# First pass of a two-layer encoder: tokens transposed by products with a diagonal of their roots, c spread from eight columns

## The chip, the cores and the metric

The kernel runs on one core of one Trainium2 chip. The metric is the device time in microseconds of one execution, from a set of three runs; lower is better. One execution was also taken by the hardware profiler, which gives the rows quoted here.

Five engines of the core work side by side, each in the order of its own queue: TensorE (PE in the rows; PEld is its weight load), VectorE (DVE), ScalarE (ACT), GpSimd (POOL), and SyncE (SP), whose queue issues nearly all the DMAs.

## The reference

A trunk of two layers over 1024 tokens of width 1024, in f32. Layer 0 is a differential attention, layer 1 a latent attention. Each layer is modulated by a vector c. What matters here is how a layer begins:

```python
def _rmsnorm(x, g):
    xf = x.astype(jnp.float32)
    y = xf * lax.rsqrt(jnp.mean(xf * xf, axis=-1, keepdims=True) + RMS_EPS)
    return (y * g.astype(jnp.float32)).astype(x.dtype)

def _modulation(c, ada_w, ada_b):
    mod = jax.nn.silu(c) @ ada_w + ada_b
    shift, scale, gate = jnp.split(mod[:, None, :], 3, axis=-1)
    return shift, scale, gate

for i in range(DEPTH):
    shift, scale, gate = _modulation(c, ada_w[i], ada_b[i])
    h = _rmsnorm(x, norm_g[i]) * (1.0 + scale) + shift
    y = mixer_i(h, ...)          # begins with proj = h @ w_in
    x = x + gate * y
return _rmsnorm(x, final_norm_g)
```

Each token of x is multiplied by its own root, `y = rsqrt(mean(x^2) + eps)`, then each feature by `a = g * (1 + scale)`, and `b = shift` is added. The change touches only how h of layer 0 comes about.

## The kernel before

Tokens lie on partitions when x is loaded (`xs0`: four tiles of 128 tokens x 1024 features, the first half of the tokens; `xs1`: the second half). The products need h with features on partitions, so x goes through TensorE in eight chunks of 128 features. `h_chunk` (L478) makes one chunk for 512 tokens: four transposes into one PSUM bank (`trh`, or `trc` in a wide bank), then ScalarE reads the bank twice, as `h * a + b` rounded to the short format of the products (`h0h`) and once more in f32, and GpSimd subtracts the two to get the remainder `h0l` (in the second half VectorE makes the f32 copy). Every f32 product is done as three products of such pairs (high x high, high x low, low x high).

The work at the start, in stages:

- **The vector c.** It is loaded as one row (`crow`, L565), goes through tanh on ScalarE and one step on VectorE (L600, L601), and is spread over all partitions by two products with a row of ones into the PSUM bank `cb` (L605). `keep_busy` (L559) issues products of ones with ones before and after it: 8, then 9 (`WARM`, L64).
- **The modulation.** For chunk k, `mod_pair` (L441) has VectorE multiply two loaded tiles of the ada weight (512 KB each, tag `ada`, four slots) with `cb` and sum each over its row; a third small step (L447) makes `a = (a + 1) * g`.
- **The roots.** The squares of the four x tiles are summed on ScalarE and VectorE, GpSimd takes the power, and ScalarE scales the first 256 columns of each x tile in place (L618, L621; `X_CUT`). VectorE scales the other 768 columns later (`x_rest`, L623), two tiles behind the modulation of chunk 0 and two behind that of chunk 1.
- **The first pass** (loop at L661, k from -1 to 8): `h_chunk` of chunk k stands ahead of the 15 products of chunk k - 1 (`SKEW`): eight for v with h0h, two for k, then five with h0l. The sums stay in the banks `vacc` and `kacc`. In between VectorE works out the rotary angles and ScalarE their sines.
- **The q strip** (L736): 24 products for the first half of the tokens; its bank comes free when the first `vacc` has been stored (L375: a ScalarE copy and a VectorE subtraction).
- **The second pass** (loop at L741): the second half of the tokens, whose four x tiles were scaled in place by `norm_x` (L468) and L730 to L733; `h_chunk` runs three chunks ahead (`SKEW1`) of twelve products per chunk.

The order on each engine is mostly that of the program; `tc.issue_after(x)` puts instructions behind x on their engine. The weights of v, k and q arrive in f32 and are split into high (ScalarE) and low (GpSimd or VectorE) parts as they are needed.

Of the kernel before, what the change touches and what calls it, by code (L numbers as in the profile page):

```python
# [11 lines left out]
F32 = mybir.dt.float32  # L12
# [9 lines left out]
P = 128  # L22
# [9 lines left out]
_W = [("norm_g0", KT), ("ada_bsh0", KT), ("ada_bsc0", KT), ("norm_g1", KT), ("ada_bsh1", KT),  # L32
      ("ada_bsc1", KT), ("subln_g", 1), ("q_a_norm_g", 3), ("kv_a_norm_g", 2), ("inv", 1), ("ada_bg0", KT), ("ada_bg1", KT)]
VEC, NVEC = {}, 0
# [27 lines left out]
X_ACT0 = (0, 2)  # L62
X_CUT = 256
WARM = (8, 9)  # L64
SIN_AT = (4, 5, 7)
# [16 lines left out]
def trunk(ctx: ExitStack, tc: tile.TileContext, A, out):  # L82
# [358 lines left out]
    def mod_pair(l, j, ws, c_):  # L441

        g, bsh, bsc, a_, b_ = mods[l]
        js = slice(j, j + 1)
        mod_dot(ws[0], bsh[:, js], b_[:, js], c_)
        mod_dot(ws[1], bsc[:, js], a_[:, js], c_)
        return V.scalar_tensor_tensor(out=a_[:, js], in0=a_[:, js], scalar=1.0, in1=g[:, js], op0=ALU.add, op1=ALU.mult).ins  # L447

# [28 lines left out]

    def h_chunk(l, xn4, k, dst, hp, sub=G, wide=False, act=False, f32=None):  # L478

        _, _, _, a_, b_ = mods[l]  # L480
        if wide:
            tr = bank("cb", "trc", [P, D])[:, :HF].rearrange("p (j q) -> p j q", j=4)
        else:
            tr = bank("tr", "trh", [P, 4, P])
        for j in range(len(xn4)):
            nk = KT // len(xn4[j])
            PE.transpose(tr[:, j, :], xn4[j][k // nk][:, (k % nk) * P : (k % nk + 1) * P], ident)
# [4 lines left out]
        h_chunk.act = S.activation(hh, tr[:, :n, :], AF.Identity, bias=bk, scale=ak).ins  # L492
# [69 lines left out]

    crow = p1.tile([P, D], F32, name="crow", tag="ada", bufs=ADA_B)
    th = p1.tile([P, D], F32, name="cth", tag="ada", bufs=ADA_B)
    SP.dma_start(crow[0:1, :], A["c"])  # L565
    xs0 = [load_x(0, 0)]
# [32 lines left out]

    c_act = S.activation(th[0:1, :], crow[0:1, :], AF.Tanh, scale=0.5).ins  # L600
    c_last = V.scalar_tensor_tensor(out=crow[0:1, :], in0=th[0:1, :], scalar=1.0, in1=crow[0:1, :], op0=ALU.add, op1=ALU.mult).ins  # L601
    cb = bank("cb", "cb", [P, D])
    for f in range(2):
        fs = slice(f * HF, f * HF + HF)
        spread = PE.matmul(cb[:, fs], ones[0:1, :], crow[0:1, fs], start=True, stop=True).ins  # L605
    with tc.issue_after(spread):
        keep_busy(WARM[1])
    c2 = pg.tile([P, D], F32, name="c2")

    y0 = [None] * 4  # L610
    ss0 = sm.tile([P, 4], F32, name="xss")
# [4 lines left out]
    for j in range(3):  # L616
        y0[j] = y_[:, j : j + 1]
        S.mul(xs0[j][0][:, :X_CUT], xs0[j][0][:, :X_CUT], y0[j])  # L618
    sq_halves([xs0[3][0][:, :HF], xs0[3][0][:, HF:]], ss0[:, 3:4])
    y0[3] = inv_rms(ss0[:, 3:4], 1)[:, 0:1]  # L620
    h_chunk.act = S.mul(xs0[3][0][:, :X_CUT], xs0[3][0][:, :X_CUT], y0[3]).ins  # L621

    def x_rest(j):  # L623
        V.tensor_scalar(xs0[j][0][:, X_CUT:], xs0[j][0][:, X_CUT:], y0[j], None, op0=ALU.mult)

# [35 lines left out]
    for k in range(-1, KT + SKEW):  # L661
        if k + 1 < KT:
# [12 lines left out]
            if k >= 0:  # L675
                with tc.issue_after(m_last):
                    next(angle_steps, None)
        if k < 0:
            with tc.issue_after(m_last):
                x_rest(0)  # L680
                x_rest(1)
        if k == 0:
            with tc.issue_after(m_last):
                x_rest(2)
                x_rest(3)
        if k == X1_AT:
# [8 lines left out]
        if 0 <= k < KT:  # L695
            h_chunk(0, xs0, k, h0[k][0], p1, act=True)
            if k % 4 == 0:
# [25 lines left out]
    with tc.issue_after(h_chunk.act):  # L723
        for j in range(2):
# [3 lines left out]
            V.tensor_add(ssb[:, j : j + 1], ssb[:, j : j + 1], sx)  # L728
    norm_x(ssa, xs1[:2])
    yb = inv_rms(ssb, 2)  # L730
    for j in range(2):
        V.tensor_scalar(xs1[2 + j][0], xs1[2 + j][0], yb[:, j : j + 1], None, op0=ALU.mult)
        S.mul(xs1[2 + j][1], xs1[2 + j][1], yb[:, j : j + 1])  # L733
    load_tables()
# [6 lines left out]
    for k in range(KT + SKEW1):  # L741
        if k < KT:
            if 0 < k <= MODS_K:
                next(mods_g)
            with tc.issue_after(q_split), tc.issue_after(q_mm):
                h_last = h_chunk(0, xs1, k, h0[k][1], p1, V if k in HL_V else G, k % 2 == 1)
        if k >= SKEW1:
# [1684 lines left out]
def layout(inputs):  # L2432
# [4 lines left out]
    def cols(v, n):  # L2437
        return ca(v.reshape(n, P).T)
# [66 lines left out]
```

## Time and profile before

| what | value |
|---|---|
| median of three runs | 1381.4 us (1381.4 to 1382.1) |
| the profiled execution | 1382.89 us |
| its span, first to last instruction | 1380.9 us |
| TensorE busy in the span | 1361.0 us (99%) |
| VectorE, ScalarE, GpSimd busy | 949.2, 738.3, 708.7 us |
| mean granted TensorE clock | 0.995 |
| first product of the first pass | 14.94 us |
| last product of the first pass begins | 48.96 us |
| q strip begins | 50.19 us |
| last transposes before the second pass begin | 55.77 us |
| next strip after the second pass begins | 82.38 us |

The last five rows are from the timeline. A row of the timeline has the start, the duration in us, engine, line, operation, output and input tiles with their shape, a count where like instructions were merged, and in brackets the idle time before it with what ended it. Durations of products overlap: two 128x512 products that each last 0.39 us can start 0.23 us apart. A busy TensorE is therefore not proof of a TensorE at its peak, and the granted clock has to be read beside it.

### The profile page before, as it was taken

To read this page: it belongs to the slowest core of one execution; us is meant where nothing else is said; L and a number is where in the kernel's file an instruction comes from. 1 tells how busy PE (TensorE), PEld (TensorE's weight loads), DVE (VectorE), ACT (ScalarE), POOL (GpSimd) and SP (SyncE) were. 2 spreads that over 40 slices of the span, in tenths; PEclk is the share of its full clock that TensorE was granted. 3 is DMA by queue.
4 is the path that set the end of the run, shared out by engine and by line. 5 is a ranking of instruction groups with operands and counts; after the bars stand their busy time and mean duration, and the time that the engine had idled before them with its cause. 6 is when DMAs were issued, how large, how long until landed. Compare 5 with 4: busy or idle time off the path is not lost.

```text
span 1380.9 us, 20717 instructions
## 1 busy us (share of the span) xinstructions
PE 1361.0 (99%) x7322; PEld 1144.8 (83%) x7322; DVE 949.2 (69%) x1334; ACT 738.3 (53%) x1357; POOL 708.7 (51%) x556
## 2 busy tenths in 40 slices
PE   8999999999999999999999999999999999999997
PEld 6788888888888888887887887788888888888886
DVE  7764788877777767778597987645566555555584
ACT  5633465565655656566648543345454454455554
POOL 4425163647585757565695135532141373834673
PEclk8999999999999999999999999999999999999999
DMA  9867644353444444526654255599343463576373
GB/s 335 275 177 222 211 108 143 113 146 103 156 114 149 135 122 130 153 71 204 210 202 170 60 160 183 161 284 286 115 117 111 111 214 123 190 222 229 118 264 122
DMA packets 149386, 232.06 MB, mean 168 GB/s; under 512 B 20641, under 2 KB 57633, under 8 KB 149282
## 3 DMA queue, kind: packets, MB, share of 16 engines
q1 hardware_dynamic: 149138, 230.48, 53.4%
q8 instruction: 57, 0.93, 0.3%
q14 instruction: 47, 0.39, 0.1%
q10 hardware_dynamic: 144, 0.26, 0.1%
HBM read 144.74 MB, written 61.81 MB: 150 GB/s over the span
## 4 chain that ended last, share of the span: by engine, by line
PE 88%; DVE 4%; DMA 2%; ACT 2%; issue 1%; POOL 1%; SPq 0%; POOLq 0%; DVEq 0%; ACTq 0%
PE s L2109 10%; PE acc L173 9%; PE acc L175 9%; PE acc L174 9%; PE tr L398 8%; PE s L869 8%; PE pv L173 4%; PE pv L174 4%; PE pv L175 4%; PE oy L173 2%; PE oy L174 2%; PE oy L175 2%; PE vps L173 2%; PE vps L174 2%; PE vps L175 2%; PE zacc L175 1%
## 5 line engine op out<-in xcount | busy, mean ns | idle before, releaser
L400 ACT CAST pth<-tr 128x512 fp32r<-128x512 f32 x256 | 150.2, 587 | 279.2 <-PE tr L398 276.3
L401 DVE TENSOR_TENSOR ptl<-tr,pth 128x512 fp32r<-128x512 f32 x256 | 176.3, 689 | 144.6 <-ACT pth L400 143.9
L415 DVE TENSOR_REDUCE nm<-s 128x1 f32<-128x1024 f32 x192 | 234.0, 1219 | 53.7 <-PE s L869 42.9
L219 POOL TENSOR_TENSOR wl<-wraw,wh 128x512 fp32r<-128x512 f32 (+2 forms) x73 | 93.4, 1280 | 264.4 <-ACT wh L218 185.8
L417 ACT ACTIVATE e<-s,nm 128x1024 f32<-128x1024 f32 x128 | 143.7, 1122 | 35.0 <-DVE nm L415 34.4
L398 PE MATMUL tr<-ident,e 128*128 128x128 f32 x1024 | 154.8, 273 | 1.8 <-DVE ptl L401 1.5
L398 PEld LDWEIGHTS tr<-ident,e 128*128 128x128 f32 x1024 | 121.3, 140 | 42.5 <-DVE ptl L401 19.7
L173 PE MATMUL acc<-h0h,wh 128*128 128x512 f32 x360 | 149.5, 415 | 0.0
L173 PE MATMUL pv<-pth,vt 128*128 128x256 f32 x512 | 147.6, 288 | 0.0
L174 PE MATMUL pv<-ptl,vt 128*128 128x256 f32 x512 | 145.4, 284 | 0.0
L175 PE MATMUL pv<-pth,vt 128*128 128x256 f32 x512 | 144.6, 282 | 0.0
L175 PE MATMUL acc<-h0h,wl 128*128 128x512 f32 x360 | 142.0, 394 | 0.0
L174 PE MATMUL acc<-h0l,wh 128*128 128x512 f32 x360 | 141.4, 393 | 0.0
L174 PEld LDWEIGHTS pv<-ptl,vt 128*128 128x128 f32 x512 | 97.5, 190 | 2.5
L1203 POOL TENSOR_TENSOR wol<-wol,woh 128x512 fp32r<-128x512 f32 x56 | 81.9, 1486 | 34.0 <-ACT woh L1202 31.8
L173 PEld LDWEIGHTS pv<-pth,vt 128*128 128x128 f32 x512 | 97.2, 190 | 2.5
L175 PEld LDWEIGHTS pv<-pth,vt 128*128 128x128 f32 x512 | 97.4, 190 | 0.0
L869 PE MATMUL s<-ks,qa 128*128 128x512 f32 x256 | 82.7, 402 | 1.3 <-DVE e L877 1.2
L877 DVE SCALAR_TENSOR_TENSOR e<-s,z,e 128x1024 f32<-128x1024 f32 x64 | 82.2, 1284 | 2.2
L175 PEld LDWEIGHTS acc<-h0h,wl 128*128 128x128 f32 x360 | 67.6, 188 | 14.7
L869 PE MATMUL s<-ks,qb 128*128 128x512 f32 x256 | 79.6, 392 | 0.0
L174 PEld LDWEIGHTS acc<-h0l,wh 128*128 128x128 f32 x360 | 68.2, 189 | 9.2
(433 smaller groups left out, 3416.8 us busy)
## 6 DMA issues: line engine op xcount, KB each, us to landing
ada<-in_ada_ss SPq DMA_DIRECT2D x32, 512.0 KB, 6.1
vS<-v_hl SPq DMA_DIRECT2D x32, 512.0 KB, 5.5
vt<-vS SPq DMA_DIRECT2D x32, 512.0 KB, 4.6
wraw<-in_w_s SPq DMA_DIRECT2D x60, 256.0 KB, 2.8
wol<-tS SPq DMA_DIRECT2D x56, 256.0 KB, 5.3
tS<-ob SPq DMA_DIRECT2D x48, 256.0 KB, 2.2
rp_sw<-rp_raw SPq DMA_DIRECT2D x160, 64.0 KB, 2.0
bc_s<-bc_d SPq DMA_DIRECT2D x34, 256.0 KB, 4.0
```

Of the source, the lines that this page charges most:

```text
L173: PE.matmul(psum, ah, bh, start=first, stop=False, skip_group_check=skip)
L174: PE.matmul(psum, ah, bl, start=False, stop=False, skip_group_check=skip)
L175: mm3.last = PE.matmul(psum, al, bh, start=False, stop=last, skip_group_check=skip).ins
L219: sub = (V if pair_of else G).tensor_sub(l_[:, :n], raw[:, :n], f32v(h_[:, :n]))
L398: transpose_p.last = PE.transpose(tr[:, j, :], p[:, kt * P : (kt + 1) * P], ident).ins
L400: mk["S"] = S.copy(pth[kh][:, :, dst], tr).ins
L401: mk["V"] = V.tensor_sub(ptl[kh][:, :, dst], tr, f32v(pth[kh][:, :, dst])).ins
L415: mk["V"] = V.reduce_max(nm, s_ps, axis=AX.X, negate=True).ins
L417: mk["S"] = S.activation(e, s_ps, AF.Exp, bias=nm, scale=1.0, accum_out=zs).ins
L869: PE.matmul(s_ps[:, kc * HF : (kc + 1) * HF], src[:, c, ql], KS[h][kc][:, c, :], start=fst, stop=not fst)
L877: combined.append(V.scalar_tensor_tensor(out=e0, in0=e1, scalar=z1[:, 0:1], in1=e0, op0=ALU.mult, op1=ALU.add).ins)
L2109: PE.matmul(s_ps[:, kc * HF : (kc + 1) * HF], lhs, rhs(kc), start=i == 0, stop=i == 4)
```

## The change

The constant `c` joins the small vectors that are loaded together as eight columns (`vec`), so its own DMA goes. Its tanh and the step after it work on 128x8 elements. VectorE then scales the identity with each of the eight columns, and TensorE multiplies ones with each of these diagonals, which spreads 128 values of c over all partitions at a time. The second run of `keep_busy` grows from 9 to 15.

x is no longer scaled. In its place ScalarE scales the identity with the roots of each tile of tokens (`diag`, into `dg0` and `dg1`), and `h_chunk` multiplies x with that diagonal instead of transposing it with the identity: the product transposes and scales at once. This is done in both halves of the tokens. `x_rest`, the ScalarE scalings and the `norm_x` of the second half go.

The small step `a = (a + 1) * g` goes from VectorE to ScalarE, as `a * g + g` (`mod_scale`), ahead of each `h_chunk`. After the first chunk's products, three products of ones with ones are issued into `kacc`, which its first real product overwrites.

```diff
-      ("ada_bsc1", KT), ("subln_g", 1), ("q_a_norm_g", 3), ("kv_a_norm_g", 2), ("inv", 1), ...
+      ("ada_bsc1", KT), ("subln_g", 1), ("q_a_norm_g", 3), ("kv_a_norm_g", 2), ("c", KT), ("inv", 1), ...
-X_CUT = 256
-WARM = (8, 9)
+WARM = (8, 15)
+KEEP0 = 3
...
     def mod_pair(l, j, ws, c_):
-        g, bsh, bsc, a_, b_ = mods[l]
+        _, bsh, bsc, a_, b_ = mods[l]
         js = slice(j, j + 1)
         mod_dot(ws[0], bsh[:, js], b_[:, js], c_)
-        mod_dot(ws[1], bsc[:, js], a_[:, js], c_)
-        return V.scalar_tensor_tensor(out=a_[:, js], in0=a_[:, js], scalar=1.0, in1=g[:, js], op0=ALU.add, op1=ALU.mult).ins
+        return mod_dot(ws[1], bsc[:, js], a_[:, js], c_).ins
+
+    def mod_scale(l, j):
+        g, _, _, a_, _ = mods[l]
+        js = slice(j, j + 1)
+        S.activation(a_[:, js], a_[:, js], AF.Identity, bias=g[:, js], scale=g[:, js])
...
-    def h_chunk(l, xn4, k, dst, hp, sub=G, wide=False, act=False, f32=None):
+    def h_chunk(l, xn4, k, dst, hp, sub=G, wide=False, act=False, f32=None, dg=None):
...
-            PE.transpose(tr[:, j, :], xn4[j][k // nk][:, (k % nk) * P : (k % nk + 1) * P], ident)
+            piece = xn4[j][k // nk][:, (k % nk) * P : (k % nk + 1) * P]
+            if dg is None:
+                PE.transpose(tr[:, j, :], piece, ident)
+            else:
+                h_chunk.tr = PE.matmul(tr[:, j, :], piece, dg[:, j, :], start=True, stop=True).ins
...
-    crow = p1.tile([P, D], F32, name="crow", tag="ada", bufs=ADA_B)
-    th = p1.tile([P, D], F32, name="cth", tag="ada", bufs=ADA_B)
-    SP.dma_start(crow[0:1, :], A["c"])
+    cd = p1.tile([P, KT, P], F32, name="cd", tag="ada", bufs=ADA_B)
+    th, cs = [sm.tile([P, KT], F32, name="cth") for _ in range(2)]
...
-    c_act = S.activation(th[0:1, :], crow[0:1, :], AF.Tanh, scale=0.5).ins
-    c_last = V.scalar_tensor_tensor(out=crow[0:1, :], in0=th[0:1, :], scalar=1.0, in1=crow[0:1, :], ...).ins
+    c_act = S.activation(th, part("c"), AF.Tanh, scale=0.5).ins
+    V.scalar_tensor_tensor(out=cs, in0=th, scalar=1.0, in1=part("c"), op0=ALU.add, op1=ALU.mult)
     cb = bank("cb", "cb", [P, D])
-    for f in range(2):
-        fs = slice(f * HF, f * HF + HF)
-        spread = PE.matmul(cb[:, fs], ones[0:1, :], crow[0:1, fs], start=True, stop=True).ins
+    for k in range(KT):
+        c_last = V.tensor_scalar(cd[:, k, :], ident, cs[:, k : k + 1], None, op0=ALU.mult).ins
+        spread = PE.matmul(cb[:, k * P : k * P + P], ones, cd[:, k, :], start=True, stop=True).ins
...
+    dg0 = p1.tile([P, 4, P], F32, name="dg", tag="dg", bufs=1)
+
+    def diag(dst, y):
+        return S.mul(dst, ident, y).ins
...
     for j in range(3):
-        y0[j] = y_[:, j : j + 1]
-        S.mul(xs0[j][0][:, :X_CUT], xs0[j][0][:, :X_CUT], y0[j])
+        diag(dg0[:, j, :], y_[:, j : j + 1])
     sq_halves([xs0[3][0][:, :HF], xs0[3][0][:, HF:]], ss0[:, 3:4])
-    y0[3] = inv_rms(ss0[:, 3:4], 1)[:, 0:1]
-    h_chunk.act = S.mul(xs0[3][0][:, :X_CUT], xs0[3][0][:, :X_CUT], y0[3]).ins
-
-    def x_rest(j):
-        V.tensor_scalar(xs0[j][0][:, X_CUT:], xs0[j][0][:, X_CUT:], y0[j], None, op0=ALU.mult)
+    h_chunk.act = diag(dg0[:, 3, :], inv_rms(ss0[:, 3:4], 1)[:, 0:1])
...
-        if k < 0:
-            with tc.issue_after(m_last):
-                x_rest(0)
-                x_rest(1)
-        if k == 0:
-            with tc.issue_after(m_last):
-                x_rest(2)
-                x_rest(3)
...
         if 0 <= k < KT:
-            h_chunk(0, xs0, k, h0[k][0], p1, act=True)
+            mod_scale(0, k)
+            h_chunk(0, xs0, k, h0[k][0], p1, act=True, dg=dg0)
+            if k == 0:
+                with tc.issue_after(h_chunk.tr):
+                    for _ in range(KEEP0):
+                        PE.matmul(kacc[:, 0:P], ones, ones, start=True, stop=True)
...
-    norm_x(ssa, xs1[:2])
+    ya = inv_rms(ssa, 2)
     yb = inv_rms(ssb, 2)
-    for j in range(2):
-        V.tensor_scalar(xs1[2 + j][0], xs1[2 + j][0], yb[:, j : j + 1], None, op0=ALU.mult)
-        S.mul(xs1[2 + j][1], xs1[2 + j][1], yb[:, j : j + 1])
+    dg1 = p1.tile([P, 4, P], F32, name="dg", tag="dg", bufs=1)
+    for j in range(4):
+        diag(dg1[:, j, :], (ya, yb)[j // 2][:, j % 2 : j % 2 + 1])
...
-                h_last = h_chunk(0, xs1, k, h0[k][1], p1, V if k in HL_V else G, k % 2 == 1)
+                h_last = h_chunk(0, xs1, k, h0[k][1], p1, V if k in HL_V else G, k % 2 == 1, dg=dg1)
...
+    small["c"] = cols(I["c"], KT)
```

More of the change, by code (lines that the diff above doesn't have):

```diff
@@ L32 @@
 _W = [("norm_g0", KT), ("ada_bsh0", KT), ("ada_bsc0", KT), ("norm_g1", KT), ("ada_bsh1", KT),
-      ("ada_bsc1", KT), ("subln_g", 1), ("q_a_norm_g", 3), ("kv_a_norm_g", 2), ("inv", 1), ("ada_bg0", KT), ("ada_bg1", KT)]
+      ("ada_bsc1", KT), ("subln_g", 1), ("q_a_norm_g", 3), ("kv_a_norm_g", 2), ("c", KT), ("inv", 1), ("ada_bg0", KT), ("ada_bg1", KT)]
 VEC, NVEC = {}, 0
@@ L598, in trunk @@
     angle_steps = angles()
-    c_act = S.activation(th[0:1, :], crow[0:1, :], AF.Tanh, scale=0.5).ins
-    c_last = V.scalar_tensor_tensor(out=crow[0:1, :], in0=th[0:1, :], scalar=1.0, in1=crow[0:1, :], op0=ALU.add, op1=ALU.mult).ins
+    c_act = S.activation(th, part("c"), AF.Tanh, scale=0.5).ins
+    V.scalar_tensor_tensor(out=cs, in0=th, scalar=1.0, in1=part("c"), op0=ALU.add, op1=ALU.mult)
     cb = bank("cb", "cb", [P, D])
-    for f in range(2):
-        fs = slice(f * HF, f * HF + HF)
-        spread = PE.matmul(cb[:, fs], ones[0:1, :], crow[0:1, fs], start=True, stop=True).ins
+    for k in range(KT):
+        c_last = V.tensor_scalar(cd[:, k, :], ident, cs[:, k : k + 1], None, op0=ALU.mult).ins
+        spread = PE.matmul(cb[:, k * P : k * P + P], ones, cd[:, k, :], start=True, stop=True).ins
     with tc.issue_after(spread):
@@ L608, in trunk @@
     c2 = pg.tile([P, D], F32, name="c2")
-    y0 = [None] * 4
+    dg0 = p1.tile([P, 4, P], F32, name="dg", tag="dg", bufs=1)
+    def diag(dst, y):
+        return S.mul(dst, ident, y).ins
     ss0 = sm.tile([P, 4], F32, name="xss")
```

## The prediction

> **What bounds the kernel now.** All that is edited runs in the first 83 us of a 1380.9 us span, so I read that stage. First the view of the waits' chain for 0 to 100 us, because it says which work ended last at each point (columns: start us, us, what).
>
> ```profile
> 2.90 6.97 DMA xt<-in_x
> 9.93 7.53 DMA ada<-in_ada_ss
> 17.49 1.28 DVE ada L439
> 18.81 0.99 DVE moda L447
> ...
> 49.55 0.60 DVE v_hl L378
> 50.19 0.50 PE acc L173
> ```
>
> See that the chain is input DMA until 17.49, then almost only VectorE, and TensorE from 50.19 on. Then the table of stretches, by stage: first pass, q strip, second pass (columns: stretch, length, busy us and count of PE, weight loads, DVE, ACT, POOL; granted clock; DMA share; GB/s).
>
> ```profile
> 14.94:49.20 34.26, 34.16 (x148) 27.13 (x148) 32.92 (x54) 20.46 (x33) 22.41 (x18) 0.91 0.94 332
> 50.19:55.77 5.58, 5.58 (x24) 4.57 (x25) 3.86 (x9) 4.37 (x11) 0.85 (x2) 1.00 0.76 203
> 55.77:82.21 26.44, 25.94 (x129) 21.09 (x127) 15.87 (x22) 9.37 (x15) 8.67 (x6) 1.00 0.69 209
> ```
>
> In the first pass TensorE and VectorE are both full, and TensorE has a clock of 0.91. In the second pass TensorE alone is full, at clock 1.00: whatever is added to it there is added to the time. The last chunk of the first pass, and the only breaks of TensorE between the passes and around the second one, from the timeline:
>
> ```profile
> 45.79 0.39 PE L712 MATMUL vacc<-wvh,h0h 128*128 128x512 f32 x1
> ...
> 48.96 0.39 PE L718 MATMUL kacc<-h0l,wh 128*128 128x512 f32 x1
> 50.19 0.50 PE L173 MATMUL acc<-h0h,wq 128*128 128x512 f32 x1 [0.84 <-DVE v_hl L378]
> 57.24 0.50 PE L173 MATMUL vacc<-wvh,h0h 128*128 128x512 f32 x1 [0.43 <-ACT h0h L492]
> 82.38 0.50 PE L173 MATMUL acc<-h0h,wq 128*128 128x512 f32 x1 [0.24 <-DVE v_hl L378]
> ```
>
> The first two rows, 14 steps apart, give the spacing of full-clock products: 3.17 / 14 = 0.226 us.
>
> **The clock.** Cutting the start into stretches of 3.41 us, the spacing at which the granted clock is seen to switch (columns as above):
>
> ```profile
> 0.54:3.95 3.41, 2.90 (x13) 2.90 (x14) 0.53 (x4) 2.34 (x2) 0.50 (x2) 1.00 0.41 106
> 3.95:7.36 3.41, 2.86 (x12) 1.42 (x11) 1.70 (x2) 1.15 (x2) 0.00 (x0) 1.00 0.98 383
> 7.36:10.78 3.42, 3.41 (x17) 3.11 (x15) 1.40 (x6) 1.87 (x4) 0.02 (x1) 0.50 1.02 412
> 10.78:14.20 3.42, 1.31 (x4) 0.55 (x4) 3.11 (x8) 2.31 (x6) 1.60 (x3) 1.00 1.04 405
> 14.20:17.61 3.41, 2.67 (x8) 2.28 (x9) 3.29 (x5) 2.38 (x4) 3.00 (x3) 0.50 1.04 407
> 17.61:21.02 3.41, 3.41 (x9) 2.64 (x8) 3.38 (x7) 1.13 (x2) 2.17 (x2) 0.50 1.03 360
> 21.02:24.43 3.41, 3.41 (x18) 2.79 (x17) 3.38 (x8) 1.18 (x3) 2.55 (x2) 1.00 0.93 312
> ```
>
> Each stretch's clock follows the busy time of the one before: full after 2.90 or 3.41, half after 1.31 (four transposes), still half after 2.67 (some of it transposes); half also after 2.86, of which 1.98 was the c spread from one row. From 14.2 to 21.0 the first chunk's products run at half clock. Later in the kernel two more pairs bound what keeps the clock (PE only: length, busy, clock, DMA share, GB/s):
>
> ```profile
> 847.04:850.45 3.41, 2.13 (x8) 1.00 0.43 161
> 1372.69:1376.10 3.41, 1.25 (x11) 1.00 0.56 208
> 1376.10:1379.51 3.41, 0.00 (x0) 0.50 0.80 297
> ```
>
> After 1.25 busy (37%) the clock falls; after 2.13 (62%) it stays, as no later stretch before 1376 shows less than 1.00.
>
> **What the change costs: products for transposes.** The same shape as the new product (f32, 128x128, a diagonal streamed) is in L926. The price is the time that it takes from its neighbours, against four transposes:
>
> ```profile
> 22.45 0.60 PE L487 MATMUL trh<-ident,xt 128*128 128x128 f32 x4
> 22.81 0.48 PE L713 MATMUL vacc<-wvl,h0h 128*128 128x512 f32 x1
> 23.13 0.39 PE L712 MATMUL vacc<-wvh,h0h 128*128 128x512 f32 x1
> ...
> 1304.75 1.05 PE L926 MATMUL rb<-dg,ones 128*128 128x128 f32 x8
> 1305.56 0.48 PE L173 MATMUL oy<-woh,oah 128*128 128x512 f32 x1
> 1305.87 0.40 PE L174 MATMUL oy<-wol,oah 128*128 128x512 f32 x1
> ```
>
> Four transposes are 4 instructions, four f32 products 8. The third row less one spacing (0.23) less the first: 23.13 - 0.23 - 22.45 = 0.45 us, and 1305.87 - 0.23 - 1304.75 = 0.89. So +0.44 per set of four, eight sets in each pass: +3.5 us of TensorE in each.
>
> Second pass: +3.5, less two breaks that it fills. h0h at 57.24 waits 0.43 behind two sets already issued, and the longer second set fills that; the 0.24 at 82.38 goes, since v_hl comes no later while TensorE does. Net 3.52 - 0.67 = **+2.85**. The norm that goes (products of x with its root on VectorE and ScalarE) lies beside the q strip, which ran to 55.77 without a break, and is worth nothing; the four ScalarE diagonals in its place lie there too.
>
> **First pass, the start.** c comes with vec, so the crow DMA and its issue go, and x is issued 0.33 us earlier; with DMA at 383 to 412 GB/s from 4 us on, all that follows lands about 0.35 earlier. The chain from there:
>
> ```profile
> 1.18 0.33 SPq L565 DMA_DIRECT2D crow<-in_c  x1
> ...
> 11.29 1.28 DVE L439 CUSTOM_DVE_ANT_0 ada<-ada,cb,vec 128x1024 f32<-128x1024 f32 x1 [0.24 <-DMA ada<-in_ada_ss]
> 14.11 0.78 ACT L492 ACTIVATE h0h<-trh,modb,moda 128x512 fp32r<-128x512 f32 x1 [0.23 <-DVE moda L447]
> 14.94 0.80 PE L712 MATMUL vacc<-wvh,h0h 128*128 128x512 f32 x1 [1.18 <-ACT h0h L492]
> 17.27 1.27 POOL L219 TENSOR_TENSOR wl<-wraw,wh 128x512 fp32r<-128x512 f32 x1
> ```
>
> mod_scale moves to ScalarE: 0.2 us there (L952, 128x4: 206 ns) for a VectorE step of 0.16 at 13.85, so even. It waits there for moda, with h0h, h and the next casts queued behind it, but h0h at their head waited for moda already; first product at 14.94 - 0.35 = 14.6. cd holds one ada slot where crow and cth held two, so chunk 1's first ada tile is issued sooner, into DMA queues that are full anyway: nothing. The c spread (eight scalings of 128 columns, above the 0.17 of 128x2 and below the 0.28 of 128x256: I take 0.21, between them, 1.7 in all) begins once vec is there, and is no bound, as ada lands only at 11.27; the eight products, 0.22 each and waited for by the fillers behind them on TensorE's queue, keep pace with it. At either end, 1.4 or 2.2, it is done well before 11.27. The diagonals (0.33 each by L925's 1.4 for four, where the 256-column scalings took 0.44) are ready by 12.6, and h0h waits for moda, not for them.
>
> VectorE loses x_rest and L447:
>
> ```profile
> L439 DVE CUSTOM_DVE_ANT_0 ada<-ada,cb,vec 128x1024 f32<-128x1024 f32 x16 | 20.0, 1274 | 0.7 <-ACT c L637 0.4 <-DMA ada<-in_ada_ss 0.2
> L447 DVE SCALAR_TENSOR_TENSOR moda<-moda,vec 128x1 f32<-128x1 f32 x8 | 4.1, 507 | 0.3
> L624 DVE TENSOR_SCALAR xt<-xt,rq_y 128x768 f32<-128x768 f32 x4 | 3.5, 883 | 0.0
> L925 ACT ACTIVATE dg<-ident,zz 128x128 f32<-128x128 f32 x4 | 1.4, 397 | 0.2 <-DVE zz L2262 0.2
> L952 ACT ACTIVATE sl_w<-zz 128x4 f32<-128x4 f32 x16 | 3.3, 206 | 0.5
> ```
>
> That is 7.6 of its 32.9 us, so it bounds no more; TensorE is late next. Its order: chunk 0 at 14.6; kacc's second product waits for wl, POOL's third job there (18.54 now, about 18.0 then, its two jobs before starting sooner); chunk 1 waits for moda of the ada tile issued at 9.93, which lands about 17.1, so h0h about 19.4. With a full clock chunk 1 starts at 19.5. With half clock until 17.6, those 3.0 us do 1.5 us of the 15 x 0.226 + 0.89 = 4.3 that chunk 0 and the next set hold, and the other 2.8 end at 20.4. Then 7 chunks x 15 x 0.226 = 23.7, and 6 sets x 0.89 = 5.3: end at 48.5 or 49.4 (now 49.2). q then waits only for ScalarE's copy and VectorE's subtraction of the first vacc, about 0.5 after the end, VectorE being free: 49.0 or 49.9, where it is 50.19 now. I take the middle, 49.5, **-0.7**.
>
> Which clock: eight first products as now (full at 3.95), spread and 15 fillers at full clock (0.22 each, 23 in all from 4.2, three instructions after 3.95) end near 9.2; 7.36 to 10.78 is then 54% busy, and 10.78 to 14.20 holds one set (0.89) and the three fills (0.67), 46%. Both lie between the 37% that lost the clock and the 62% that kept it, so both outcomes are priced; at 88% busy from 14.6 it should be back by 17.6. The Trainium skill, page "TensorE: Matmul & The Clock Gate", Part 1, says that the clock drops only after an idle window, which would give 19.5 and a sum lower by 0.4. The 1.25-us stretch above, not idle and yet followed by half clock, speaks against it.
>
> The fills (0.67) and longer warming lie before 14.6 where TensorE has nothing else; if the diagonals came later than 13.5 they would cost up to 0.67.
>
> **Sum.** -0.7 + 2.85 = +2.15 on the span of 1380.9. The profiled run was 1382.89, 1.5 above the median of three runs (1381.4); I add to the median: **1383.6**. Its own range is +1.4 to +3.0: both clocks, and stalls up to 0.5. After 82 us everything waits relative to TensorE's progress, so the delay stays.
>
> **Rivals.**
> Slower: the clock stays half until 21.0 as now, because transitions at 10.78 and 17.61 both go against it. The 6.4 us to 21.0 then do 3.2 of the 4.3, chunk 1 starts at 22.1 instead of 19.9 to 20.0, so +2.2: 1385.8. It decides if 14.2 to 17.6 stays under some 80% busy (2.67 of 3.41 was not enough, 2.90 was). For: waits for wvl and wl there. Against: products count where transposes seem not to. Chance 0.20.
>
> The early gain doesn't come: another feeder than VectorE (ScalarE's table load and sines, wvr landing late; DMA share is 0.94) holds q at 50.2: +2.85, 1384.3. Against: ScalarE is busy 20.5 of 34.3. Chance 0.15.
>
> Faster: a product costs TensorE no more than a transpose here. The first pass then ends at 19.9 + 23.7 + 6 x 0.45 = 46.3, q at 46.8 (-3.4), and the second pass gains 0.24: 1377.8. L926's eight instructions speak against it. Chance 0.07.
>
> Dearer products: at four times a transpose, a set is 1.80, 16 x 1.35 = 21.6 more than 0.45, so about 1401; against it L926's 0.89. Chance 0.02. The Trainium skill's same page, Terms, gives transpose mode as four times faster for FP32; L926 shows two.
>
> A shift that later stages turn into another order of waits, either way by 3 us: 0.06. My forecast keeps 0.50.
>
> **Chances.** A measurement can tell about 0.2% (2.8 us) from no change. Above 1384.2: all but 0.01 of the slower clock (0.19), half of the lost gain (0.08), a fifth of the forecast (0.10), dear products (0.02), late order (0.02): 0.41. Below 1378.6: 0.07 + 0.02 = 0.09. Rest 0.50. The range, 1380.8 to 1386.6, leaves out the faster rival, the dear products and most of the late order.
>
> **What would show it.** Products on trh in pairs, 0.89 per set; clock 1.00 from 17.6 at the latest; first q product near 49.5; from the first set of the second pass to its last vacc product 26.44 + 3.1; VectorE idle at times in 20 to 45 us. It would be wrong if sets take 0.45, if the clock is half at 20, or if the second pass isn't without breaks.

## The result, and the profile after

The changed kernel takes **1393.4 us** (median of six runs, 1393.1 to 1394.5), the kernel before 1381.4 in the same set: ratio 1.0087, 95% interval 1.0074 to 1.0100, so 12.0 us slower. The profiled execution has a span of 1391.6 us against 1380.9. The forecast was 1383.6 with a range up to 1386.6: the sign was right, but most of the loss was not foreseen. One run of e1 below (1934 us, the profiled one) and one of e4 (1866 us) were in a slower state, with a mean granted clock of 0.65 and 0.68, and no time below counts them.

The stretches of the changed kernel, to be read beside the table of the prediction (columns as there: stretch, length, busy us and count of PE, weight loads, DVE, ACT, POOL; granted clock; DMA share; GB/s):

```profile
14.24:48.49 34.25, 34.22 (x176) 28.52 (x176) 29.65 (x45) 23.31 (x40) 22.91 (x19) 1.00 0.97 355
49.09:52.50 3.41, 0.49 (x2) 0.44 (x3) 1.25 (x5) 3.41 (x11) 0.17 (x1) 1.00 0.94 224
52.50:55.92 3.42, 3.42 (x11) 2.64 (x10) 2.35 (x4) 1.48 (x4) 0.54 (x1) 0.52 1.15 267
52.01:59.26 7.25, 7.25 (x25) 5.80 (x26) 2.70 (x6) 1.97 (x5) 0.70 (x1) 0.76 1.06 275
59.26:88.77 29.51, 29.51 (x162) 25.32 (x161) 17.83 (x23) 10.86 (x16) 9.55 (x7) 1.00 0.44 143
```

First row: the first pass, from 14.24 to its end at 48.5, at clock 1.00 (0.91 before). The last row is the second pass, 29.51 us without a break (82.38 less 55.77, 26.61, before). Both came out as forecast. Between them lies what was not: TensorE does almost nothing in 49.09 to 52.50, the next 3.41 us have half the clock (0.52 in the row, since the clock itself switches at 52.67), and the q strip takes 7.25 us instead of 5.58. TensorE's timeline there (start us, us, what, idle time before it and what ended it):

```profile
48.29 0.39 PE L722 MATMUL kacc<-h0l,wh 128*128 128x512 f32 x1
52.01 0.50 PE L173 MATMUL acc<-h0h,wq 128*128 128x512 f32 x1 [3.34 <-DVE v_hl L378]
```

It waits 3.34 us for VectorE's subtraction of the first vacc, which waits for ScalarE's copy. ScalarE's timeline:

```profile
45.96 0.63 ACT L539 ACTIVATE junk<-xth 128x512 bf16<-128x512 f32 x1 [1.20 <-DMA xth<-in_x]
...
48.85 0.40 ACT L621 ACTIVATE dg<-ident,rq_y 128x128 f32<-128x128 f32 x1 [2.17 <-POOL rq_y L169]
49.16 0.61 ACT L539 ACTIVATE junk<-xth 128x512 bf16<-128x512 f32 x1
...
49.77 0.39 ACT L621 ACTIVATE dg<-ident,rq_y 128x128 f32<-128x128 f32 x1
50.06 0.61 ACT L539 ACTIVATE junk<-xth 128x512 bf16<-128x512 f32 x1
...
50.67 0.56 ACT L377 CAST v_hl<-vacc 128x512 fp32r<-128x512 f32 x1
```

The copy (last row) could have run from about 47.8 (in e9 below it starts 0.5 us ahead of the first pass's last product). Ahead of it in ScalarE's queue stand the first diagonal of the second half, which waits for GpSimd's power until 48.85, another diagonal, and two squares. In the kernel before the same copy ran at 48.48, and all four squares stood behind it. ScalarE's timeline there:

```profile
48.48 0.59 ACT L377 CAST v_hl<-vacc 128x512 fp32r<-128x512 f32 x1 [2.74 <-PE vacc L717]
48.97 0.63 ACT L530 ACTIVATE junk<-xth 128x512 bf16<-128x512 f32 x1
```

Where the time went can be followed by how far each TensorE product lies behind the same one of the kernel before: 0.7 us ahead at 48.3, 1.8 behind at the q strip's start, 3.5 at the second pass's start (59.26 less 55.77), 6.4 at its end (88.77 less 82.38), and 8.5 at the first product of s (147.00 less 138.50). Of the last step 1.74 is one wait:

```profile
92.30 0.50 PE L173 MATMUL acc<-h0h,wh 128*128 128x512 f32 x1 [1.74 <-DVE v_hl L378]
```

and VectorE's timeline shows what the subtraction stood behind: the lam multiplication, whose DMA had not landed. In the kernel before all four subtractions come ahead of it.

```profile
91.42 0.23 DVE L848 TENSOR_TENSOR lam<-lam 128x64 f32<-128x64 f32 x1 [1.83 <-DMA lam<-in_lam]
91.56 0.68 DVE L378 TENSOR_TENSOR v_hl<-vacc,v_hl 128x512 fp32r<-128x512 f32 x1
```

The other 2 us or so of the loss come in small steps after 147 us.

### The profile page after: what moved, and what is told of

It reads as the page before. It is cut to its first block, busy times and chain, and to the rows that moved or that the text cites. A ratio compares the mean times of both kernels' runs of the same rounds, so it can differ in the third digit from the quotient of the medians.

```text
span 1391.6 us, 20920 instructions
## 1 busy us (share of the span) xinstructions
PE 1371.4 (99%) x7416; PEld 1154.5 (83%) x7416; DVE 941.8 (68%) x1326; ACT 740.5 (53%) x1367; POOL 707.1 (51%) x556
## 4 chain that ended last, share of the span: by engine, by line
PE 88%; DVE 4%; DMA 2%; ACT 2%; issue 2%; POOL 1%; SPq 1%; POOLq 0%; DVEq 0%; ACTq 0%
PE s L2113 10%; PE acc L173 9%; PE acc L175 9%; PE acc L174 9%; PE s L873 8%; PE tr L398 8%; PE pv L173 4%; PE pv L175 4%; PE pv L174 4%; PE oy L173 2%; PE oy L175 2%; PE oy L174 2%; PE vps L173 2%; PE vps L174 2%; PE vps L175 2%; PE zacc L175 2%
## 5 line engine op out<-in xcount | busy, mean ns | idle before, releaser
L344 POOL TENSOR_TENSOR rp_sw<-rp_sw,sinT 128x512 f32<-128x512 f32 x40 | 53.6, 1340 | 50.3 <-DMA rp_sw<-rp_raw 49.9
```

## The experiments

All times are medians; the last column is (ratio to the kernel before - 1) x 1381.4 us, with the interval's ends, so that runs of different sets can be compared.

| kernel | median us | us over the kernel before |
|---|---|---|
| changed kernel | 1393.4 | 12.0 (10.2 to 13.8) |
| e3 lam behind | 1391.5 | 9.7 (7.9 to 11.3) |
| e12 lam behind, pause filled | 1389.2 | 7.7 (6.1 to 9.4) |
| e1 copy first | 1388.5 | 6.8 (4.8 to 8.6) |
| e2 second half transposed | 1387.8 | 5.4 (3.5 to 7.3) |
| e4 less warming | 1395.2 | 14.1 (11.6 to 16.6) |
| e7 kernel before, tiles shifted | 1385.3 | 3.9 (2.3 to 5.2) |
| e10 changed, tiles in place | 1393.4 | 9.9 (7.7 to 12.3) |
| e11 tiles in place, lam behind | 1388.6 | 6.5 (4.7 to 8.3) |
| e9 tiles in place, copy first | 1384.8 | 2.9 (1.7 to 4.0) |
| e6 second half transposed, copy first, lam behind | 1387.7 | 5.7 (3.9 to 7.5) |
| e8 as e6, tiles in place | 1384.5 | 2.8 (1.7 to 4.0) |
| e15 as e8, norm behind | 1385.6 | 3.6 (2.1 to 5.0) |
| e13 kernel before, warming | 1386.8 | 5.4 (3.3 to 7.3) |
| e14 as e13, copy first, norm behind | 1383.4 | 1.4 (0.1 to 2.6) |
| e16 kernel before, copy first, norm behind | 1382.1 | 0.3 (-1.0 to 1.5) |

Two theories stood against each other. **Order:** the loss is the order of instructions on ScalarE and VectorE around the q strip, and the clock that the pause costs. **Price:** the products with diagonals cost more than forecast.

### The order: e1 and e3

e1 puts the copy of the first vacc ahead; squares and diagonals go behind it:

```diff
-    with tc.issue_after(h_chunk.act):
+    store_v(0, p1b, vacc[0], 0, 0)
+    v_first = store_v.act
+    with tc.issue_after(v_first):
         ...
-    for j in range(4):
-        diag(dg1[:, j, :], ...)
+    with tc.issue_after(v_first):
+        for j in range(4):
+            diag(dg1[:, j, :], ...)
...
-    for tt in range(4):
+    for tt in range(1, 4):
         store_v(0, p1b, vacc[tt], tt, 0)
```

> Computes what the changed kernel computes; only the order of issue on ScalarE differs: the copy of the first vacc goes ahead of the four squares and the four diagonals of the second half. Order theory (the q strip is late because the first vacc copy stands behind two diagonals that wait for GpSimd's power, the 3.5 us pause then costs the clock, and the lam multiplication in front of the fourth subtraction costs 1.7 more): first q product near 49.0, clock 1.00 through the q strip (5.6 us long instead of 7.4), no wait of 1.7 at 92; some 5 to 6.5 us below the changed kernel's 1393.4, so 1387 to 1388.5. The second pass then may wait for its first diagonals at its start, by up to 1 us. Price theory (the products themselves make up nearly all of the loss, and the order only moves a wait about): within 1.5 us of the changed kernel, 1392 to 1394.

It took 1388.5, 5.2 us less than the changed kernel by the ratios, as the order theory has it. Of its trace only the order is read: the copy stands ahead of the squares, and lam falls behind the four subtractions by itself, so lam's wait is part of the 5.2. e9 below has the same order, with times.

e3 moves the lam multiplications alone:

```diff
-    for i in range(2):
-        V.tensor_mul(lam4[:, 2 * i, :], ...)
-        V.reduce_sum(lp[:, i : i + 1], ...)
+    with tc.issue_after(store_v.sub):
+        for i in range(2):
+            ...
```

> One edit to the changed kernel: the two lam multiplications and sums are issued on VectorE behind the last vacc subtraction that was issued before them. Order theory: TensorE's wait of 1.74 us for v_hl at 92.3 goes, nothing else does: 1.7 us less, 1391.7. Rival: what waits behind is released by something as late (the lam transfer is only a neighbour), so 1393.4 within 0.4.

1391.5: 1.9 us less by the medians, 2.3 by the ratios. The wait is gone from its timeline, and the first product of s comes at 144.89 instead of 147.00.

### The clock: e12, e4, e13

e12 is e3 with TensorE kept busy in the pause, with products whose results nobody uses:

```diff
+    for _ in range(14):
+        PE.matmul(h_chunk.tile[:, 0, :], ones, ones, start=True, stop=True)
     ssa, ssb = ...
```

> The kernel with the lam multiplications behind (1391.5), and 14 products of ones with ones (0.22 us each, 3.1 in all, results unused) on TensorE behind the first pass's last product, in the pause before the q strip; a few products of the second pass change places with transposes beside them. It isolates the clock: TensorE gains nothing but being busy. Clock theory: the q strip begins at about 52.0 as it does there, but takes 5.6 us instead of 7.4 at clock 1.00, so 1.8 less, 1389.5 to 1390. If the half clock is not the pause's doing, or the wait for the next copies takes its place: 1391.5 within 0.5.

TensorE's timeline of e12:

```profile
48.62 3.29 PE L724 MATMUL trh<-ones 128*128 128x128 f32 x28
51.66 0.48 PE L173 MATMUL acc<-h0h,wq 128*128 128x512 f32 x1
...
57.35 0.61 PE L496 MATMUL trh<-dg,xt 128*128 128x128 f32 x4
```

The q strip starts 0.23 us earlier than in e3 (51.89) and ends after 5.69 us, the first set of the second pass less its start; in e3 it takes 7.26 (to 59.15). 1389.2 against 1391.5: 2.0 us by the ratios, for work that computes nothing, and no run of one lies among those of the other (1388.4 to 1389.7, and 1390.5 to 1392.0). So half the clock after the pause is a cost of its own, beside the pause.

e4 takes the change's warming away (`WARM = (8, 9)`, `KEEP0 = 0`):

> The changed kernel without the later warming: 9 in place of 15 late fillers and no fills in the first chunk. It computes the same. If the warming keeps the clock, as the forecast left open: the clock is half in part of the first two chunks, the first pass ends up to 0.9 us later, and the q strip up to 0.9 later: 1393.4 to 1394.5. If ScalarE's order sets the q strip's start (the order theory), TensorE's end can move by 0.9 without the q strip moving: the same time within 0.3 though the first pass ends later.

1395.2 (1393.5 to 1399.5), 2 us more than the changed kernel by the ratios. That would be more than either theory gave, but the runs overlap those of the changed kernel (1393.1 to 1394.5), so it is not clear of noise. Its clock record shows half from 10.8 to 17.7, from 51.8 to 58.6 and again from 96.2 to 99.6. The first of these is what the forecast left open; the q strip moved with the first pass's end (49.32 for its last product, 52.71 for q), against what I had expected from the order theory, since the squares and diagonals ahead of the copy moved along.

e13 adds the same warming to the kernel **before**, and nothing else:

> The kernel before with the warming alone: 15 late fillers instead of 9, and three fills behind the first chunk's transposes. Tokens, transposes, c spread and places stay as they were (15 us of the first pass at half clock in the profile of before, 14.2 to 21.0). If the warming holds the clock: no half-clock stretch after 11 us, the first pass ends up to 1.5 us earlier, so 1380 to 1381, and the times spread less than the 1380.2 to 1384.4 of the kernel before. If not: 1381.7 within 0.5.

(The "15 us" in it is a slip; 14.2 to 21.0 are 6.8 us.) The opposite came out: 1386.8, 5.4 us slower, with runs from 1382.7 to 1389.3. The first pass does end 1.3 us earlier, but the q strip starts 0.7 later than in the kernel before. TensorE's row, from the profiled run, which was the fastest of the six:

```profile
50.90 0.50 PE L174 MATMUL acc<-h0h,wq 128*128 128x512 f32 x1 [2.84 <-DVE v_hl L379]
```

VectorE's timeline of e13:

```profile
48.76 1.42 DVE L477 TENSOR_SCALAR xt<-xt,rq_y 128x1024 f32<-128x1024 f32 x2 [0.82 <-POOL rq_y L170]
50.09 0.15 DVE L733 TENSOR_TENSOR xss<-xss,xs 128x1 f32<-128x1 f32 x1
50.16 1.28 DVE L379 TENSOR_TENSOR v_hl<-vacc,v_hl 128x512 fp32r<-128x512 f32 x2
```

Here two norm multiplications of the second half's tokens (1.42) stand ahead of the subtraction, and wait for GpSimd too. In the kernel before the subtraction came first. The edit adds products on TensorE only, and yet the order on VectorE came out the other way round. That the earlier end of the first pass did this is argued, not shown.

The same run shows how the clock can outlast such a pause. Cut along the 3.41-us grid of its own clock record:

```profile
45.91:49.32 3.41, 2.15 (x10) 1.46 (x8) 2.55 (x6) 3.13 (x9) 0.71 (x1) 1.00 1.03 382
49.32:52.73 3.41, 1.83 (x8) 1.52 (x9) 2.56 (x8) 1.67 (x5) 0.70 (x1) 1.00 0.99 245
```

The pause of 2.84 us is split over two stretches of the grid, 63% and 54% busy, and the clock stays. In e11 (below) a pause of 2.82 falls into one:

```profile
49.14:52.55 3.41, 0.59 (x3) 0.47 (x3) 1.29 (x5) 3.41 (x11) 0.20 (x1) 1.00 0.64 190
52.55:55.96 3.41, 3.41 (x9) 2.67 (x9) 2.31 (x4) 1.44 (x4) 0.50 (x1) 0.50 1.11 247
```

17% busy, and half the clock follows. The grid lies differently against the program in each execution (it switches at 3.95 us in the profile of before and at 4.95 in e13's), so the same pause can keep the clock in one run and cost it in the next. That fits the spread of e13's times. One stretch at half clock lowers a run's mean clock by 0.0012 (half of 3.41 us in 1383), and the mean granted clock was 0.999 in the profiled run and 0.996 or 0.997 in the five slower ones. Which stretches these lost is not known, as only the fastest run has a profile.

### The place of the tiles: e2, e7, e10, e11, e9, e6, e8

e2 has the second half back to scaled tokens and transposes:

```diff
-    ya = inv_rms(ssa, 2)
+    norm_x(ssa, xs1[:2])
     yb = inv_rms(ssb, 2)
-    dg1 = p1.tile([P, 4, P], F32, name="dg", tag="dg", bufs=1)
-    for j in range(4):
-        diag(dg1[:, j, :], (ya, yb)[j // 2][:, j % 2 : j % 2 + 1])
+    for j in range(2):
+        V.tensor_scalar(xs1[2 + j][0], xs1[2 + j][0], yb[:, j : j + 1], None, op0=ALU.mult)
+        S.mul(xs1[2 + j][1], xs1[2 + j][1], yb[:, j : j + 1])
...
-                h_last = h_chunk(0, xs1, k, ..., dg=dg1)
+                h_last = h_chunk(0, xs1, k, ...)
```

> The second half goes back to scaled tokens and transposes, the first half keeps the products. Order theory: the second pass gets its 2.7 us back, and the two diagonals' wait for GpSimd's power no longer stands ahead of the first vacc copy, though three squares still do: q strip at 49.5 to 51, 4 to 7 us below the changed kernel, so 1386 to 1389. Price theory: the products of the second pass and what hangs on them are nearly all of the loss, so back to 1381 to 1384 whatever the order on ScalarE.

1387.8, in the order theory's bounds and 4 us above those of the price theory. But its profile raised a question: at the end of the second pass TensorE is only 0.4 us behind the profile of before (82.78 against 82.38), and at the end of the span 5.3. So something that has nothing to do with the passes costs time later.

The later code is the same, but not where its tiles lie. `vec` has eight columns more, and the new `cth` tiles take four buffers of 32 bytes per partition in a pool that stays open to the end: 32 + 128 = 160 bytes, by which all tiles of the left pools behind them move. e7 makes this shift in the kernel before, with its unused tile:

```diff
-PADL = 96 // 4
+PADL = 256 // 4
```

> The kernel before with one constant changed: the unused tile padl is 256 bytes per partition instead of 96. All tiles of the left pools behind it lie 160 bytes further, as they do in the changed kernel (vec has eight columns more, and the two cth tiles take four buffers of 32 bytes each). No instruction differs. Place theory (the drift of some 2 to 5 us that TensorE collects after 100 us in the changed kernel and in the kernel with the second half transposed comes from where the tiles lie): products of s from ks and qb are 0.234 apart instead of 0.228, and the time is 2 to 5 us above the kernel before, 1383.5 to 1386.5. Rival (the drift comes from the changed first part, through the order of the work that follows): 1381.4 within 1, products 0.228 apart.

1385.3: 3.9 us (2.3 to 5.2) for no changed instruction. The products of s in 138 to 400 us, grouped by line (count, busy us, mean ns of one), in the kernel before and then in e7:

```profile
L869 PE MATMUL s<-ks,qb 128*128 128x512 f32 x125 | 38.8, 391 | 0.0
```

```profile
L869 PE MATMUL s<-ks,qb 128*128 128x512 f32 x124 | 38.8, 394 | 0.0
```

And from TensorE's timeline the first and the 127th product of s from qa, again before and then e7:

```profile
138.50 0.39 PE L869 MATMUL s<-ks,qa 128*128 128x512 f32 x1
...
402.14 0.39 PE L869 MATMUL s<-ks,qa 128*128 128x512 f32 x1
```

```profile
138.56 0.39 PE L869 MATMUL s<-ks,qa 128*128 128x512 f32 x1
...
403.44 0.40 PE L869 MATMUL s<-ks,qa 128*128 128x512 f32 x1
```

That is 3 ns more for one product and 1.24 us more between the two rows (264.88 against 263.64). This distance divides all profiled kernels: 264.8 to 264.9 us in the changed kernel, e2, e3, e4, e6, e7 and e12, which are all shifted; 263.1 to 263.8 in the kernel before, e8 to e11 and e13 to e16, which are not.

The other way round, e10 is the changed kernel with the shift undone:

```diff
-PADL = 96 // 4
+PADL = 64 // 4
...
-    th, cs = [sm.tile([P, KT], F32, name="cth") for _ in range(2)]
+    th, cs = [p1.tile([P, KT], F32, name="cth", tag="cth", bufs=2) for _ in range(2)]
```

> The changed kernel with the tiles of the attention stage where they lay before: the cth tiles come from the pool of the first pass and padl is 64 bytes instead of 96. Nothing else differs. Place theory: 2 to 5 us below the changed kernel, 1388.5 to 1391.5, with 0.228 between s products, and the first 90 us as they were. Rival: 1393.4 within 1.

The products are fast again (263.7 between the two rows), yet five of six runs took 1392.4 to 1394.2, like the changed kernel, and one 1387.5. The profile shows why: the wait behind lam is now 2.65 us, and lies so that the clock falls a second time.

```profile
88.80:92.20 3.40, 1.07 (x5) 0.56 (x3) 0.71 (x3) 2.42 (x4) 1.27 (x1) 1.00 0.84 238
92.20:95.62 3.42, 3.11 (x7) 2.51 (x8) 2.25 (x8) 0.20 (x1) 0.00 (x0) 0.50 1.14 336
```

The run of 1387.5 has a mean clock of 0.998 and the other five 0.996 or 0.997, which fits a drop less in that run; it has no profile. e11, e10 with lam behind, removes the cause:

> The changed kernel with the tiles of the attention stage where they lay before and the lam multiplications behind the vacc subtractions; ScalarE's order is the changed kernel's. With the place alone mended the clock fell to half a second time, in 92 to 96 us, behind the wait for the fourth subtraction, and the time stayed at 1393.4 (1387.5 in one run). If that second drop ate the gain: no wait at 92, no second half-clock stretch, and 1388 to 1389.5. If the place is worth nothing once the first part is changed: 1391.5, as with the lam multiplications alone.

1388.6, against 1391.5 for e3, the same kernel shifted: 3.2 us by the ratios, and no second drop. e9 has the copy first and the shift undone, with the products in both halves:

> Products in both halves, the copy of the first vacc ahead on ScalarE, and the tiles of the attention stage where they lay before. Order and place theories together: 1389.0 (the copy ahead alone) less 2 to 5, so 1384 to 1387, which is the second pass's 2.7 and little more over the kernel before; q strip at 49 with clock 1.00. If the place is worth nothing: 1389 within 1.

1384.8, 3.9 us below e1 by the ratios. From its timeline of ScalarE and then of TensorE:

```profile
48.06 0.59 ACT L377 CAST v_hl<-vacc 128x512 fp32r<-128x512 f32 x1 [4.12 <-PE vacc L721]
48.54 0.63 ACT L539 ACTIVATE junk<-xth 128x512 bf16<-128x512 f32 x1
49.08 0.19 ACT L539 ACTIVATION_READ_ACCUMULATOR junk<-xth 128x1 f32 x1
49.17 0.39 ACT L621 ACTIVATE dg<-ident,rq_y 128x128 f32<-128x128 f32 x1
```

```profile
49.43 0.50 PE L173 MATMUL acc<-h0h,wq 128*128 128x512 f32 x1 [0.50 <-DVE v_hl L378]
```

And its stretches, q strip and second pass:

```profile
49.43:55.00 5.57, 5.57 (x24) 4.61 (x25) 3.58 (x8) 4.88 (x14) 0.71 (x1) 1.00 0.72 203
55.00:84.32 29.32, 29.32 (x161) 25.24 (x160) 18.07 (x22) 10.15 (x15) 10.50 (x7) 1.00 0.68 196
```

This is the first part as it was forecast: q at 49.43, the strip 5.57 long at full clock, with the diagonals beside it, the second pass 29.3 from its first set to the next strip. There, at 84.32, TensorE is 1.94 us behind the kernel before, where the forecast had 2.15. That q came within 0.1 us of the 49.5 is partly luck: 49.5 was the middle between 49.0 for a full clock and 49.9 for a half one, and the clock was full. lam falls behind the subtractions by itself here.

e6 and e8 transpose the second half, have the copy first and lam behind; e6 is shifted, e8 is not:

> The changed kernel with the second half scaled and transposed as before, the copy of the first vacc ahead of the four squares on ScalarE, and the lam multiplications behind the vacc subtractions. Order theory: the q strip begins at 49.0 to 49.4, 1.5 us earlier than with the second half transposed alone (50.76), so about 1386.4 if the later drift (some 5 us in that kernel) stays, and about 1381 if it goes with the order. Price theory: same as with the second half transposed alone, 1387.8.

> The first half by products as in the changed kernel, the second half scaled and transposed as before, the copy of the first vacc ahead on ScalarE, the lam multiplications behind the vacc subtractions, and the tiles of the attention stage where they lay before. Theory (order, clock, place and the second pass's 2.7 us are the whole loss): all four are gone, so the kernel before within 1 us, 1380.5 to 1382. Against its twin without the place mended (1387.7) that is 6, more than the 3.5 that the shift alone cost the kernel before; if only 3.5 come back, 1384, and 2.5 us have another cause in the transposed second half.

1387.7 and 1384.5: 2.9 us by the ratios for the place, for the fourth time (3.9, 3.9, 3.2, 2.9). The fifth pair, the changed kernel and e10, gives 2.1, with the second drop of the clock in it. But e6 is not below e2, and e8 is 2.8 us above the kernel before where I expected none. The order is again part of it: in e8 the q strip starts at 50.60, after a wait of 1.93, since on VectorE the two norm multiplications (1.42) stand ahead of the subtraction, as in e13 (and in e2, where the wait is 1.78).

### What was left: e15, e14, e16

e15 is e8 with `norm_x` of the second half issued behind the first subtraction:

```diff
-    norm_x(ssa, xs1[:2])
+    with tc.issue_after(v_sub):
+        norm_x(ssa, xs1[:2])
```

> The kernel with the second half transposed, copy ahead, lam behind and places restored (1384.45), and in it the two norm multiplications of the second half's tokens on VectorE behind the first vacc subtraction. There the q strip still waited 1.93 us, because the two multiplications (1.42) stood ahead of the subtraction. Order theory: q strip at about 49.0, 1.6 less, 1382.5 to 1383.2; what then is left over the kernel before lies behind 400 us (a wait for qb at 411 and one for ptl at 1196, some 0.8 each). If the first half's products cost something that I haven't seen: 1384.4 within 0.5.

The q strip starts at 49.48, near the 49.0 expected, but the time is 1385.6, no better than e8 and not the 1382.5 to 1383.2 expected. The norm, put back, is late in its turn for the second pass's transposes, which then delay h0h too (TensorE's timeline):

```profile
56.33 0.33 PE L494 MATMUL trh<-ident,xth 128*128 128x128 f32 x1 [0.88 <-DVE xth L739]
...
57.92 0.50 PE L173 MATMUL vacc<-wvh,h0h 128*128 128x512 f32 x1 [0.65 <-ACT h0h L501]
```

e14 and e16 do the same to the kernel before, with and without the warming:

> The kernel before with the warming (1386.8, up to 1389.3, as the q strip waited 2.84 us for the first vacc subtraction and the clock fell in most runs), the first vacc copy ahead of the squares on ScalarE and its subtraction ahead of the norm multiplications on VectorE. Order and clock theory: no pause over 0.6 us before the q strip, q strip at about 48.2, two us ahead of the kernel before's profile (50.19), no half-clock stretch: 1379 to 1380.5, and the spread of its times below 2 us. If the warming itself harms: 1385 or more.

> The kernel before with the order alone changed: the first vacc copy ahead of the squares, its subtraction ahead of the norm multiplications; no warming. In the profile of before both stood in front already, so the q strip should gain only its wait of 0.84, to 0.5: 1381.4 less 0 to 0.5. If warming and order both matter on their own, this stays at 1381 and the kernel with both is below it by 1 to 2; if the order is all, the two are equal.

e16 is the kernel before within the measurement (0.3 us, -1.0 to 1.5). e14 is 1.4 above it, with runs from 1380.5 to 1387.5 where 1379 to 1380.5 was expected, so warming by itself gains nothing even with the order mended. Its stretches, along the grid of its clock, and TensorE's row show a reason in the profiled run:

```profile
20.40:23.83 3.43, 0.95 (x7) 0.39 (x6) 3.43 (x4) 0.82 (x2) 2.68 (x3) 1.00 0.78 291
23.83:27.24 3.41, 3.41 (x9) 2.73 (x10) 3.38 (x7) 0.79 (x2) 0.00 (x0) 0.50 0.34 94
```

```profile
23.82 0.47 PE L488 MATMUL trh<-ident,xt 128*128 128x128 f32 x1 [2.48 <-DVE xt L625]
```

A faster TensorE in the first chunk runs into VectorE's scaling of the tokens (`x_rest`), pauses there, and loses the clock, which in this run's record had been full only since 13.59. The change's products in the first half do remove this wait.

No version tried is faster than the kernel before.

## Why the prediction failed, point by point

- **Product price: right.** On TensorE's timeline of the changed kernel half a set stands in each row, and the rows are 0.44 and 0.45 apart, so 0.89 for a set, as forecast:

```profile
59.26 0.61 PE L496 MATMUL trh<-dg,xt 128*128 128x128 f32 x4
59.70 0.61 PE L496 MATMUL trh<-dg,xth 128*128 128x128 f32 x4
60.15 0.61 PE L496 MATMUL trc<-dg,xt 128*128 128x128 f32 x4
```

  The second pass grew by 2.9 us (2.7 in e9), forecast 2.85. The price theory falls: with order and place mended (e9) the whole change costs 2.9 us (1.7 to 4.0), and the sum of the forecast was +2.15.
- **First pass: right.** First product at 14.24 (14.6), full clock throughout, end at 48.5, the earlier of the two ends given. Two details cancel in it: TensorE has chunk 0 behind it at 19.02 and is not held to 19.5 by chunk 1's h0h (17.31, forecast about 19.4), but the rest, forecast as 23.7 + 5.3 = 29.0 us, takes 29.5.
- **"q then waits only for ScalarE's copy and VectorE's subtraction of the first vacc, about 0.5 after the end, VectorE being free": wrong, and the step that failed.** I asked whether VectorE was free and not what stood in ScalarE's queue ahead of the copy. "The four ScalarE diagonals in its place lie there too" placed them beside the q strip, where in fact two stood ahead of the copy and one of them waited for GpSimd until 48.85. The working set them at nothing, and did not ask what they wait for. q came at 52.01 instead of 49.0 to 49.9. e9 shows it, with q at 49.43; its tiles are also back in their place, but that alone leaves q at 51.72 (e10). e1 shows what the order is worth in time.
- **The clock** was priced at the start, and not at the new pause, although the 37% stretch in the prediction said what a pause does. e12 shows 2.0 us for it. The Trainium skill, page "TensorE: Matmul & The Clock Gate", Part 1, says that the window of the clock gate runs freely against the kernel, which is what e11 and e13 show for pauses of one length. Its table of states also has the clock fall after an idle window, which the prediction took as the only way; here stretches 17% (e11) and 31% busy (e10) were enough, and the measurement decides.
- **"The norm that goes [...] is worth nothing": true only for the old timing.** When the first pass ends earlier the norm stands in the way of the subtraction on VectorE (e13, e8) or is late for the transposes (e15). That is why giving the second half its transposes back gains nothing over e9, in spite of 2.7 us less on TensorE.
- **"After 82 us everything waits relative to TensorE's progress, so the delay stays": wrong twice.** lam waits for a DMA and not for TensorE, and came to stand in front of a subtraction (1.9 to 2.3 us, e3). And the later stages run slower for where their tiles lie (2.9 to 3.9 us, four pairs). Nothing in the prediction weighed the second; the change's new small tiles were priced as instructions only. The rival "a shift that later stages turn into another order of waits" was the nearest, with 0.06.

So along this path of kernels, of 12.0 us 5.2 are the order, with lam's wait and the clock (the changed kernel to e1), 3.9 the place (e1 to e9), and 2.9 what was forecast as 2.15.

**What stays open.** The trace shows 1.2 us of the place's cost between 138 and 403 us, and products slower by 3 ns; where the rest of its 3 to 4 us falls was not settled, nor why the shift slows the products. No shift other than the 160 bytes was tried. And e8 and e15, with the second pass as short as before, still take 2.8 and 3.6 us more; waits of 0.6 to 1.0 us after 400 us (for qb, ptl and o in their views of waits) are likely part of it, and were not followed further.

## What to carry to other kernels

Where a change moves the end of a stage, list the queue of every engine that the next stage's first instruction waits for, with the waits of what stands in it, and ask whether the order there was right only for the old timing. Price a pause of TensorE as the pause and the half clock after it, which depends on how the pause falls on a 3.41-us grid, so that one execution can hide it. A changed size of a long-lived tile moves all tiles behind it: undo that shift in an experiment before the change's own steps are blamed or praised.

## What the runs showed of the hardware that I had not expected

- The same products take 391 ns or 394 (means of 125 and 124) when all tiles of the left pools lie 160 bytes further, with the same instructions (the kernel before and e7). By the distance between the two rows of s, seven shifted kernels (264.8 to 264.9 us) and nine others (263.1 to 263.8) fall apart without an exception.
- The clock stayed full after stretches of the grid that were 54% (e13) busy and fell after 31% (e10), 28% (e14) and 17% (e11). In e2 a pause of 1.78 us left 1.64 us of work, 48%, in one stretch of its grid, and it stayed full. The closest two are both 45% busy: after 1.52 us of work the clock fell (e4, 92.74 to 96.15), after 1.55 us it stayed (e8, 47.13 to 50.54). Busy time alone does not tell, as the prediction's stretch of 2.86 us, most of it the c spread from one row, was followed by half clock.
- Work that computes nothing made a kernel faster (e12, 2.0 us by the ratios), and warming made one slower (e13, 5.4 us by the ratio).
